# Regrouping the RWKV layer of a two-layer decoder kernel: two head groups half a step apart in the scan, key norms four tiles at a time, and GpSimd's work moved away from the first inversion

## The chip, the cores and the metric

The kernel runs on one core of one Trainium2 chip. The metric is the device time of one execution in microseconds (us); with one core that is the time of this core. The engines are named as in the profile: PE is TensorE (PEld its weight loads), DVE is VectorE, ACT is ScalarE, POOL is GpSimd and SP is SyncE, whose queue starts most of the transfers.

## The reference

The reference is a two-layer decoder trunk on 512 tokens of 1024 values. Layer 0 mixes tokens by a gated projection and a gated recurrence and ends in a dense SwiGLU. Layer 1 is an RWKV-7 time mixing of 16 heads of 64, then a top-2-of-8 mixture of experts. The change touches the time mixing alone:

```
    r = xr @ w_r ;  k = xk @ w_k ;  v = xv @ w_v        # xr, xk, ... mix a token with the one before it
    kk = heads(k * k_k)
    kk = kk / jnp.maximum(jnp.sqrt(jnp.sum(kk * kk, axis=-1, keepdims=True)), 1e-12)
    k = heads(k * (1.0 + (a - 1.0) * k_a))
    decay = jnp.exp(-jnp.exp(heads(w_log)))
    def step(s, inp):                                   # over 512 tokens, s is 64 x 64 for each head
        r_t, w_t, k_t, v_t, kk_t, b_t = inp             # b = kk * a
        s = (s * w_t[:, :, None, :]
             - jnp.einsum('bhvk,bhk->bhv', s, kk_t)[..., None] * b_t[:, :, None, :]
             + v_t[..., None] * k_t[:, :, None, :])
        return s, jnp.einsum('bhvk,bhk->bhv', s, r_t)
    ...                                                 # group norm of y per head (ln_g, ln_b), + bonus * v
    y = (y * g) @ w_o
```

## The kernel before, in words

The kernel is one program for one core. Layer 0 comes first, the RWKV layer lies between about 560 and 1040 us of the execution, and the expert layer, which streams its weights, takes the rest. A scheduler in the framework sets each engine's order from the order in which the code is written; `after(x, y)` pins an instruction behind another.

The recurrence is done in 8 chunks of 64 tokens (NCH = 8), and the 16 heads in two groups of 8 (`hf` 0 and 1), each group being 4 tiles of 128 channels. The stages that matter here, in order:

- **Key stage.** For each of 8 key tiles (128 channels, two heads), `key1` (L779 to 795) multiplies by w_k on PE (24 matmuls of 128x512), squares the result on ACT, splits the square in a rounded and a remaining part (`hi` on ACT, `lo` on POOL, L791). `key2` (L797 to 809) sums both parts over each head with 8 small matmuls (L800) and takes the reciprocal root by a chain of small DVE and ACT instructions. `key3` (L826 to 837) spreads it back with 4 matmuls (L831) and scales the tiles on POOL (L835) and DVE (L836, L837). `bonus_z` multiplies r by k on POOL (L816), and `bonus` sums it on PE (L823). Between and behind the tiles stands the first half of the v projection (`v_mm`, L867, 24 matmuls for each of 4 quarters of the sum).
- **Flips and flops.** For every chunk but the last and each group, `flip` scales a block of keys (POOL L847, for some chunks ACT) and `flop` transposes it on PE (L853) and writes it to DRAM, from where the scan reads it (`load_kt`).
- **Scores.** `scores(th)` (L937 to 981) makes, for chunks 0 to 3 (th = 0) and 4 to 7 (th = 1) and both groups, the products within a chunk (L956) and copies them out of PSUM with a causal mask: for th = 0 by DVE multiplications (L969, L970), for th = 1 by ACT copies (L962 to 967) and three affine selects on POOL (L976).
- **Inversions.** `invert(th)` (L985 to 1007) inverts 128 triangular 32x32 blocks on DVE: a transpose (L988), then 31 columns of a multiplication (L997) and a subtraction (L1001), both with two inputs in SBUF, then two transposes (L1004, L1006). `merge1` and `merge2` (L1027 to L1044) join the blocks to 64x64 ones by small matmuls on PE.
- **Scan.** `slot(s)` (L1257 to 1274) does for every chunk four steps on PE (L1141 and L1146, L1159, L1175, L1195) with ACT and DVE copies between; DVE adds the new state (L1181, L1183 for the first chunk), and POOL multiplies it by the decay (L1188). The two groups go through a step together, group 1 one chunk behind group 0, so that there are 9 slots. Behind each step stand `fill`s: dense matmuls of other work (the second half of v, then the gate matmuls L1244 to 1246, then the output projection L1308). `norm` (L1208 to 1237) is the group norm: POOL L1224, L1215 and L1216, DVE L1218 to L1237. Its factors come by four loads of `ln_gb` (L1353), which are issued in slot 4.

## Time and profile before

| | us |
|---|---|
| median of 3 runs (1482.36 to 1485.77) | 1482.56 |
| the profiled execution's own time | 1484.26 |
| its span in the trace | 1482.6 |
| PE busy in the span | 1383.6 (93%) |
| DVE busy | 993.4 (67%) |
| ACT busy | 807.1 (54%) |
| POOL busy | 334.4 (23%) |

The profiled execution is 1.7 us above the median. The table gives shares of the whole span, and the kernel's stages differ: from the profile's slices PE is busy 9 tenths or more nearly everywhere, but falls to between 3 and 8 tenths in slices 18 to 23 (about 670 to 890 us), which hold the key stage, the scores and the inversions. The mean granted TensorE clock is 0.958 of full speed; what is missing is missing between about 740 and 960 us.

### The profile page before, as it was taken

How to read it: one execution, taken by the hardware profiler on the slowest of the kernel's cores; microseconds unless marked ns; L12 is line 12 of the kernel's file. 1: busy time of each engine (PE TensorE's matmuls, PEld its weight loads, DVE VectorE, ACT ScalarE, POOL GpSimd, SP SyncE). 2: the span in 40 equal slices, each digit the busy share in tenths (PEclk: the TensorE clock that was granted, in tenths of full speed). 3: DMA queues.
4: the chain of work that ended last, by engine and by line, in shares of the span. 5: the costliest groups of instructions: out<-in, count | busy, mean ns of one | idle time of the engine just before them, and what ended most of it. 6: DMA issues, size and time to landing. Idle time of an engine off the chain costs nothing.

```text
span 1482.6 us, 31313 instructions
## 1 busy us (share of the span) xinstructions
PE 1383.6 (93%) x12567; PEld 1090.9 (74%) x12567; DVE 993.4 (67%) x1684; ACT 807.1 (54%) x1291; POOL 334.4 (23%) x375
## 2 busy tenths in 40 slices
PE   7999999999999999999878399898989999999995
PEld 5776788888888544654445267777889999999995
DVE  6643574544444433596679965675998998898885
ACT  4841444332233332396548435354778888888872
POOL 4000002000000012202532522642324322431323
PEclk9999999999999999999988768899999999999997
DMA  4220222223223433243122124245989999999983
GB/s 172 86 72 29 86 80 92 91 93 100 99 88 98 119 102 107 60 154 114 57 71 86 45 74 132 85 161 192 368 297 371 369 406 352 373 353 399 342 331 130
DMA packets 77109, 253.39 MB, mean 171 GB/s; under 512 B 9130, under 2 KB 9258, under 8 KB 76956
## 3 DMA queue, kind: packets, MB, share of 16 engines
q1 hardware_dynamic: 69824, 232.82, 44.6%
q0 software_dynamic: 3136, 10.62, 2.4%
q10 hardware_dynamic: 3996, 7.88, 1.4%
q8 instruction: 100, 1.64, 0.5%
q14 instruction: 53, 0.43, 0.1%
HBM read 235.12 MB, written 16.16 MB: 169 GB/s over the span
## 4 chain that ended last, share of the span: by engine, by line
PE 75%; DVE 13%; issue 4%; POOL 3%; ACT 2%; DMA 2%; ACTq 0%; DVEq 0%; SPq 0%; POOLq 0%
PE ps L264 8%; PE ps L263 8%; PE ps L265 8%; PE ps L1800 7%; PE ps L1801 7%; PE ps L1799 7%; PE ps L245 3%; PE ps L247 3%; PE ps L246 3%; DVE xs L997 2%; DVE xs L1001 2%; PE ps L1308 1%; PE ps L1923 1%; PE ps L867 1%; PE ps L278 1%
## 5 line engine op out<-in xcount | busy, mean ns | idle before, releaser
L226 ACT ACTIVATE whi<-wraw 128x1024 fp32r<-128x1024 f32 x95 | 100.6, 1059 | 276.1 <-PE ps L264 125.9
L264 PE MATMUL ps<-xg,whi 128*128 128x512 f32 x544 | 216.4, 399 | 3.8 <-DVE xg L326 3.7
L263 PE MATMUL ps<-xg,whi 128*128 128x512 f32 x544 | 216.8, 399 | 1.0 <-ACT xg L325 1.0
L265 PE MATMUL ps<-xg,wlo 128*128 128x512 f32 x544 | 216.5, 398 | 0.0
L1722 DVE SCALAR_TENSOR_TENSOR wlo<-eraw,wlo 128x1024 f16<-128x1024 f32 x125 | 154.3, 1234 | 12.5 <-ACT wlo L1721 11.5
L1722 DVE SCALAR_TENSOR_TENSOR whi<-eraw,whi 128x1024 f16<-128x1024 f32 x124 | 152.6, 1231 | 14.3 <-ACT whi L1721 14.1
L227 DVE TENSOR_TENSOR wlo<-wraw,whi 128x1024 fp32r<-128x1024 f32 x95 | 118.9, 1252 | 48.6 <-ACT whi L226 47.4
L1721 ACT ACTIVATE wlo<-eraw 128x1024 f16<-128x1024 f32 x125 | 131.9, 1055 | 24.4 <-PE ps L1801 10.0
L1721 ACT ACTIVATE whi<-eraw 128x1024 f16<-128x1024 f32 x124 | 130.7, 1054 | 15.7 <-PE ps L1801 12.5
L1901 POOL TENSOR_TENSOR hh<-su,hh 128x138 f16<-128x138 f32 (+5 forms) x77 | 82.1, 1067 | 218.8 <-ACT hh L1900 216.7
L1801 PE MATMUL ps<-xe,whi 128*128 128x138 f16 (+6 forms) x704 | 126.9, 220 | 3.9 <-DVE whi L1722 2.9
L1800 PE MATMUL ps<-xe,wlo 128*128 128x138 f16 (+6 forms) x704 | 127.5, 221 | 0.5 <-issue 0.5
L1799 PE MATMUL ps<-xe,wlo 128*128 128x138 f16 (+6 forms) x704 | 127.6, 221 | 0.3 <-issue 0.3
L1799 PE MATMUL ps<-xe,whi 128*128 128x138 f16 (+6 forms) x704 | 127.7, 221 | 0.0
L1800 PE MATMUL ps<-xe,whi 128*128 128x138 f16 (+6 forms) x704 | 127.6, 220 | 0.1
L1801 PE MATMUL ps<-xe,wlo 128*128 128x138 f16 (+6 forms) x704 | 127.1, 221 | 0.4
L264 PEld LDWEIGHTS ps<-xg,whi 128*128 128x128 f32 x544 | 102.8, 189 | 31.4 <-DVE xg L326 6.5
L263 PEld LDWEIGHTS ps<-xg,whi 128*128 128x128 f32 x544 | 103.3, 190 | 25.2 <-ACT xg L325 1.4
L265 PEld LDWEIGHTS ps<-xg,wlo 128*128 128x128 f32 x544 | 103.1, 189 | 24.2 <-issue 0.5
L1801 PEld LDWEIGHTS <-whi 128*128 128x128 f16 x1008 | 98.2, 97 | 9.1 <-DVE whi L1722 5.6
L286 POOL TENSOR_TENSOR tmp<-tmp 128x512 f32<-128x512 f32 x21 | 34.5, 1641 | 302.4 <-ACT tmp L284 249.5
L1800 PEld LDWEIGHTS <-wlo 128*128 128x128 f16 x1016 | 99.3, 98 | 2.2 <-issue 2.1
(521 smaller groups left out, 3423.4 us busy)
## 6 DMA issues: line engine op xcount, KB each, us to landing
eraw<-in_e_w SPq DMA_DIRECT2D x260, 512.0 KB
wraw<-in_ffn_g SPq DMA_DIRECT2D x22, 512.0 KB
wraw<-in_ffn_u SPq DMA_DIRECT2D x22, 512.0 KB
wraw<-in_ffn_d SPq DMA_DIRECT2D x16, 512.0 KB
wraw<-in_w_oo SPq DMA_DIRECT2D x13, 512.0 KB
wraw<-in_w_mo SPq DMA_DIRECT2D x8, 512.0 KB
wraw<-in_w_rk SPq DMA_DIRECT2D x8, 512.0 KB
wraw<-in_w_k SPq DMA_DIRECT2D x8, 512.0 KB
```

The source lines that it names most:

```text
L226: nc.scalar.activation(hi, raw, AF.Copy)
L227: nc.vector.tensor_sub(lo, raw, hi.bitcast(F32))
L245: nc.tensor.matmul(ps, w[:, 0, j], xh, start=(k == 0), stop=False)
L263: nc.tensor.matmul(ps, hi[:, j], xh, start=(k == 0), stop=False)
L264: nc.tensor.matmul(ps, hi[:, j], xl, start=False, stop=False)
L265: last = nc.tensor.matmul(ps, lo[:, j], xh, start=False, stop=(k == ktot - 1))
L1721: nc.scalar.activation(w[:, 0], raw, AF.Copy, scale=2048.0)
L1722: low = nc.vector.scalar_tensor_tensor(w[:, 1], raw, 2048.0, w[:, 0], op0=OP.mult, op1=OP.subtract)
L1799: nc.tensor.matmul(ps, w[:, 0, j], x[:, 0, k], start=(k == 0), stop=False)
L1800: nc.tensor.matmul(ps, w[:, 0, j], x[:, 1, k], start=False, stop=False)
L1801: nc.tensor.matmul(ps, w[:, 1, j], x[:, 0, k], start=False, stop=(k == n - 1))
L1901: nc.gpsimd.tensor_sub(hh[:, 1, f], u, hh[:, 0, f])
```

## The change

- The squares come straight from PSUM, without the split into two parts. The sums over heads of four key tiles go into one PSUM tile (`sums`, 4 fp32 matmuls for each tile, L802 of the changed kernel), and the chain of the reciprocal root runs twice, for tiles 0 to 3 and 4 to 7.
- All 14 flips are on POOL and in the key stage or in `scores(0)`; they use the ring of two `xs` buffers that the first inversion needs, too. The flops of group 1 stand in `scores(0)` and `scores(1)`.
- The 24 affine selects of `scores(1)` are gone. In their place stand 16 multiplications by the mask on POOL (L1002, L1003), held behind the first inversion by a copy of the mask on DVE (L1116).
- The third quarter of v's first half moves into `scores(0)`, the fourth stays with `scores(1)`. Of v's second half 48 matmuls stand beside the first inversion, 16 in the first merge, and the rest at the start of the scan.
- In the scan each group goes through its step alone, group 1 half a chunk behind group 0, in 8 half-steps of a slot; the fills behind a half-step are 2, then 1 in slots 1 to 5, then 4. So the gate matmuls are used up in slots 1 and 2.
- The loads of `ln_gb` are issued in slot 1.

The diff, cut to its core:

```diff
 def key1(n):
+            nc.scalar.activation(sq, pk, AF.Square, scale=kkc[:, n:n + 1])
             nc.scalar.activation(kk, pk3, AF.Copy, scale=kkc[:, n:n + 1])
-            nc.scalar.activation(sq.rearrange("p (i s) -> p i s", i=NTT), kk, AF.Square)
-            hi, lo = xs()
-            nc.scalar.activation(hi, sq, AF.Copy)
-            nc.gpsimd.tensor_sub(lo, sq, hi.bitcast(F32))
...
+        def sums(n, pre=None):
+            g, j = divmod(n, 4)
+            if not j:
+                pqs[g] = self.ps()[:64, :128]
+            z = sqs.pop(n)
+            for i in range(NTT):
+                r0 = 8 * j + 2 * i
+                mm = nc.tensor.matmul(pqs[g], indw[:, 30 - r0:94 - r0], z[:, i * 128:(i + 1) * 128], start=(j + i == 0),
+                                      stop=(j == 3 and i == NTT - 1))
...
-                    if th:
-                        for z, j, qs in ((BS[hf][c], 0, (0, 1)), (ak.rearrange("p a b t -> p (a b) t"), 1, (e,))):
-                            for q in qs:
-                                z_ = z[64 * q:64 * q + 64]
-                                nc.gpsimd.affine_select(z_, z_, pattern=[[0, 8], [1, C]], base=-j, channel_multiplier=-1,
-                                                        compare_op=OP.is_ge, fill=0.0)
...
+        def mask(hf, c):
+            nc.gpsimd.tensor_mul(a, a, msk[nat, 1:2, :].to_broadcast([64, 8, C]))
+            nc.gpsimd.tensor_mul(z, z, msk[:, 0:1, :].to_broadcast([128, 8, C]))
...
         run(inv)
+        after(nc.vector.tensor_copy(msk, msk), inv_end[0])
         inv = invert(1)
-        run(inv, 2)
+        run(inv, 12)
+        fill(None, 48 - vdone[0])
...
-        def slot(s, gs, counts, rate):
-            chains = [(hf, s - hf) for hf in range(NH) if 0 <= s - hf < NCH]
-            for f, n in zip((step1, step2, step3, step4), counts):
-                mm = f(chains)
+        def slot(s, gs, count, rate):
+            for f, hf, c in ((step1, 0, s), (step3, 1, s - 1), (step2, 0, s), (step4, 1, s - 1),
+                             (step3, 0, s), (step1, 1, s), (step4, 0, s), (step2, 1, s)):
+                if not 0 <= c < NCH:
+                    continue
+                mm = f([(hf, c)])
...
-            slot(s, ..., ((6, 6, 4, 4), (6, 6, 4, 4), (6, 6, 4, 4), (6, 6, 4, 4), (2, 2, 1, 1), (2, 2, 1, 1), (12, 12, 0, 0), (12, 12, 0, 0), (6, 6, 0, 0))[s], (2, 2, 2, 2, 1, 1, 1, 1, 1)[s])
+            slot(s, ([inv, mk], [inv, mk], [inv, mk], [join], ...)[s],
+                 (2, 1, 1, 1, 1, 1, 4, 4, 4)[s], 1)
```

POOL before, from the last flip of the key stage on: the first inversion's fills of its tile (MEMSET xs), then selects and flips up to the second inversion's fill (cut behind the first rows).

```order
L990 MEMSET xs 128x1024
L991 MEMSET xs 128x32
L847 TENSOR_TENSOR tmp<-KB,pe 128x512
L976 AFFINE_SELECT bs<-bs 64x512 x2
L976 AFFINE_SELECT ak<-ak 64x512
```

The same place in the changed kernel: `ak` and `bs` are the masked scores, `nt` and `S` the merge's and the scan's tiles.

```order
L850 TENSOR_TENSOR xs<-KB,pe 128x512 x7
L1013 MEMSET xs 128x1024
L1014 MEMSET xs 128x32
L1129 MEMSET S 64x8x64 x4
L1055 MEMSET nt_6449 32x32x32 x2
L1055 MEMSET nt_6448 32x32x32 x2
L1002 TENSOR_TENSOR ak<-ak,msk 64x512
L1003 TENSOR_TENSOR bs<-bs,msk 128x512
L1002 TENSOR_TENSOR ak<-ak,msk 64x512
L1013 MEMSET X 128x1024
```

Between the fills of the two inversions' tiles there is no flip and no select any more; 16 mask multiplications now stand from there up to the first decay multiplication of the scan.

DVE before, in the second inversion's columns (L997 the multiplication, L1001 the subtraction; the last factor of a shape is the column's number), where the first states of the scan's group 0 are copied (L1183):

```order
L997 TENSOR_TENSOR xs<-xs,X 128x7x18 x2
L1001 TENSOR_TENSOR X<-X,xs 128x7x18 x2
L997 TENSOR_TENSOR xs<-xs,X 128x7x19
L997 TENSOR_TENSOR xs<-xs,X 128x6x19
L1183 COPY S<-ps 64x4x64 x2
L1001 TENSOR_TENSOR X<-X,xs 128x7x19
```

The same copy in the changed kernel (L1201, with L1020 and L1024 for the columns):

```order
L1020 TENSOR_TENSOR xs<-xs,X 128x5x22 x2
L1024 TENSOR_TENSOR X<-X,xs 128x5x22 x2
L1201 COPY S<-ps 64x4x64 x2
L1020 TENSOR_TENSOR xs<-xs,X 128x5x23
L1020 TENSOR_TENSOR xs<-xs,X 128x4x23
L1024 TENSOR_TENSOR X<-X,xs 128x5x23
```

It stood within column 19 and now stands behind column 22; group 1's copy now stands behind column 27.

PE before, in slots 4 and 5 of the scan: `L1141` opens a slot, `dual` names the gate matmuls.

```order
L1141 MATMUL ps<-S,RK 128x128 x8
L1146 MATMUL ps<-vu,ak 64x64 x16
L1246 MATMUL ps<-X,dual 128x512
L1244 MATMUL ps<-X,dual 128x512
L1159 MATMUL ps<-tmp,nt_6533 64x64 x16
L1245 MATMUL ps<-A_6720,dual 128x512
L1246 MATMUL ps<-X,dual 128x512
L1175 MATMUL ps<-vu,kt 64x64 x16
L1195 MATMUL ps<-vu,bs 64x64 x16
```

The same place in the changed kernel (L1159 and L1164 for L1141 and L1146, then L1177, L1193, L1213):

```order
L1193 MATMUL ps<-vu,kt 64x64 x8
L1159 MATMUL ps<-S,RK 128x128 x4
L1164 MATMUL ps<-vu,ak 64x64 x8
L1213 MATMUL ps<-vu,bs 64x64 x8
L1177 MATMUL ps<-tmp,nt_6448 64x64 x8
L1213 MATMUL ps<-vu,bs 64x64 x8
L1159 MATMUL ps<-S,RK 128x128 x4
L1164 MATMUL ps<-vu,ak 64x64 x8
```

Each step has half as many matmuls, steps of the two groups alternate, and no gate matmul stands between them.

## Rows read from the trace of the kernel before

**Rows 1.** The page: the span, and the chain of work that ended last, by engine as a share of the span.
```profile
span 1482.6 us, 31313 instructions
PE 75%; DVE 13%; issue 4%; POOL 3%; ACT 2%; DMA 2%; ACTq 0%; DVEq 0%; SPq 0%; POOLq 0%
```
**Rows 2.** Two stretches of 20 us. Columns: the stretch, its length, busy us (and instructions) of PE, PEld, DVE, ACT and POOL, the granted clock, the DMA share, GB/s.
```profile
740.00:760.00 20.00, 15.38 (x86) 8.93 (x85) 13.45 (x23) 9.01 (x20) 10.85 (x9) 0.84 0.16 53
820.00:840.00 20.00, 6.50 (x53) 4.12 (x51) 20.00 (x54) 10.20 (x32) 11.45 (x14) 0.78 0.17 65
```
**Rows 3.** The chain of waits in the key stage, in order of time: start, length, what.
```profile
730.38 2.48 POOL tmp L816 x2
732.86 1.23 POOL xs L791
...
740.77 2.47 POOL tmp L816 x2
```
**Rows 4.** PE in order of time from the last key tile to the first scores: start, length, what, and the idle time before it with its releaser.
```profile
745.58 0.95 PE L823 MATMUL ps<-indr,tmp 128*128 128x2 f32 x8
...
748.16 5.35 PE L867 MATMUL ps<-whi,xn 128*128 128x512 f16 x24
...
780.62 3.46 PE L956 MATMUL ps<-RK,KB 64*128 64x128 f32 x32
```
**Rows 5.** DVE in order of time: the first and last copies of `scores(0)`, then the first inversion's first column, one in its middle, the last one, and its last transpose.
```profile
783.61 0.42 DVE L969 TENSOR_TENSOR bs<-ps,msk 128x256 f32<-128x256 f32 x1 [0.31 <-ACT A L964]
...
797.01 0.43 DVE L970 TENSOR_TENSOR ak<-ps,msk 64x256 f32<-64x256 f32 x1
...
799.54 0.27 DVE L997 TENSOR_TENSOR xs<-xs 128x16 f32<-128x16 f32 x2
...
820.20 2.57 DVE L1001 TENSOR_TENSOR xs<-xs 128x135 f32<-128x135 f32 x2
...
841.73 0.21 DVE L1001 TENSOR_TENSOR xs<-xs 128x31 f32<-128x31 f32 x1
...
843.74 1.85 DVE L1006 STREAM_TRANSPOSE X<-xs 128x1024 f32<-128x1024 f32 x1
```
**Rows 6.** Two stretches chosen by what stands in them, columns as in rows 2: the middle of the first inversion, and the scan from the middle of slot 3 to slot 4.
```profile
810.69:833.49 22.80, 12.16 (x108) 7.75 (x105) 22.80 (x37) 17.79 (x57) 19.20 (x24) 0.95 0.19 70
```
```profile
913.00:934.00 21.00, 21.00 (x322) 19.97 (x321) 3.07 (x6) 7.27 (x12) 2.47 (x4) 0.51 0.28 90
```
**Rows 7.** DVE in order of time in the second inversion (th = 1), whose columns have the same shapes as the first one's.
```profile
849.74 1.05 DVE L997 TENSOR_TENSOR xs<-xs,X 128x16 f32<-128x16 f32 x2 [2.15 <-POOL X L991]
...
852.08 1.84 DVE L1036 COPY nt<-xs 32x1024 f32<-32x1024 f32 x2
...
863.64 0.66 DVE L1001 TENSOR_TENSOR X<-X,xs 128x135 f32<-128x135 f32 x2
...
866.62 2.80 DVE L1001 TENSOR_TENSOR X<-X,xs 128x126 f32<-128x126 f32 x2
...
882.16 0.88 DVE L1183 COPY S<-ps 64x256 f32<-64x256 f32 x2 [12.25 <-PE ps L1175]
883.07 1.16 DVE L1001 TENSOR_TENSOR X<-X,xs 128x133 f32<-128x133 f32 x2
...
892.92 0.21 DVE L1001 TENSOR_TENSOR X<-X,xs 128x31 f32<-128x31 f32 x1
```
**Rows 8.** Groups of POOL instructions between 690 and 1000 us: line, operation, tiles, shapes, count, busy us, mean ns of one, idle time before them and its releasers.
```profile
L1188 POOL TENSOR_TENSOR SP<-S,pe 64x256 f32<-64x256 f32 x24 | 18.9, 787 | 47.3 <-DVE S L1181 32.6 <-DVE S L1183 13.5
L1216 POOL TENSOR_TENSOR tmp<-tmp,xn 128x512 f32<-128x512 f32 x8 | 12.1, 1512 | 0.5
L847 POOL TENSOR_TENSOR tmp<-KB,pe 128x512 f32<-128x512 f32 x11 | 12.1, 1098 | 16.3 <-PE ps L853 11.3 <-DVE xn L712 4.7
L976 POOL TENSOR_SCALAR_AFFINE_SELECT bs<-bs 64x512 f32<-64x512 f32 x16 | 11.7, 732 | 26.7 <-ACT bs L966 25.9
```
**Rows 9.** PE in order of time in the scan: the openings of slots 1, 2, 4 and 6 (L1141; one step of the other kind, L1146, beside them), the start of the second merge (L1027), and one wait.
```profile
884.97 1.05 PE L1141 MATMUL ps<-S,RK 128*128 128x128 f32 x8
...
896.23 2.04 PE L1141 MATMUL ps<-S,RK 128*128 128x128 f32 x16 [1.15 <-DVE S L1181]
898.20 1.15 PE L1146 MATMUL ps<-vu,ak 64*64 64x64 f32 x32
...
910.04 2.11 PE L1027 MATMUL ps<-xs,A 32*32 32x32 f32 x64
...
928.32 3.78 PE L1141 MATMUL ps<-S,RK 128*128 128x128 f32 x16
...
949.44 0.69 PE L1175 MATMUL ps<-vu,kt 128*64 128x64 f32 x16 [2.66 <-ACT vu L1163]
...
952.19 3.03 PE L1141 MATMUL ps<-S,RK 128*128 128x128 f32 x16
```
**Rows 10.** The chain of waits in slots 3 to 5: start, length, what.
```profile
921.90 14.00 issue
...
937.15 1.29 POOL bs L1224
```
**Rows 11.** One group of DVE instructions of the norms between 690 and 1000 us, columns as in rows 8.
```profile
L1235 DVE TENSOR_TENSOR bs<-bs,gvar 128x512 f32<-128x512 f32 x4 | 6.3, 1586 | 0.4 <-DVE gvar L1234 0.4
```

More of the change, by code (lines that the diff above doesn't have):

```diff
@@ L777, in rwkv, with run @@
         bon = self.bon
-        prods, rns = {}, {}
+        sqs, pqs, rns = {}, {}, {}
+        def run(g, n=999):
+            for _ in range(n):
+                if next(g, "end") == "end":
+                    return
         def key1(n):
@@ L1008, in invert @@
             yield
-        def run(g, n=999):
-            for _ in range(n):
-                if next(g, "end") == "end":
-                    return
         S_ = [(b, e) for b in range(2) for e in range(2)]
@@ L1329, in out0 @@
             yield from out_mm(0, A, done)
-        load_vu(0, 0)
-        load_kt(0, 0)
-        load_kt(1, 0)
-        for mm, n in zip(merge(0), (2,) * 8):
-            fill(mm, n)
+        for hf in range(NH):
+            load_vu(hf, 0)
+            load_kt(hf, 0)
+        for mm in merge(0):
+            fill(mm, 2)
+            run(inv, 1)
         g2 = [scp.tile([128, D], F32R, name=name, bufs=2) for name in ("X", "A21")]
@@ L1341, in rwkv, with masks @@
         join = iter(())
+        def masks():
+            for c in range(4, NCH):
+                for hf in range(NH):
+                    mask(hf, c)
+                    yield
+        mk = masks()
         for s in range(NCH + 1):
-            if s == 3:
-                run(inv)
-                join = merge(1)
-            if s == 4:
+            if s == 1:
+                fill(None, 96 - vdone[0])
                 run(dense)
@@ L1353, in rwkv @@
                         nc.sync.dma_start(z[b], bass.AP(tensor=src.tensor, offset=src.offset + j * D + b * 512, ap=[[0, 128], [1, 512]]))
-                for i in (2, 3):
-                    t = self.t()
-                    nc.scalar.activation(t, pv[i], AF.Copy, scale=cm[:, 0:1])
-                    nc.sync.dma_start(v_d[i * 128:(i + 1) * 128, 512:], t)
+            if s == 3:
+                run(inv)
+                join = merge(1)
+            if s == 4:
+                run(mk)
+                run(join)
             if s == 6:
```

225 lines of the change are left out of this document (114 added, 111 removed).

## The prediction

> **What bounds the kernel now.** I read the page first, then the stretches of 20 us through the RWKV layer, then the chain of waits and each engine's order of time where a stretch showed a new limit. On the page PE holds 75% of the chain that ended last and DVE 13% [rows 1]: nearly everything is matmuls in a row, and only where PE waits for another engine is there time that a new order can win. The stretches show where. In the key stage PE is busy for 15.38 of 20 us, and in the first inversion for 6.50 of 20, with DVE at 20.00 [rows 2]. In the late key tiles the chain runs over POOL: r times k (2.48 us), then the remainder of the squares (1.23), and the next tile's pair comes 10.39 us after the last one [rows 3], while PE's own work in such a tile is 5.35 for 24 matmuls, 0.95 for the bonus [rows 4] and about half a microsecond of small ones (an estimate from these). In the first inversion the chain is DVE alone, from the first column at 799.54 to the last transpose's end at 845.59 [rows 5]. From there PE is full again, but partly at half clock: in 913 to 934 it is busy for 21.00 of 21 us at a granted clock of 0.51, its lower level of 1.2 GHz [rows 6]. Behind the scan the expert layer streams weights and only moves as a whole with the scan's end.
>
> **A. Key stage and scores: 0.** The new tile has no remainder on POOL and runs the root's chain for four tiles at once. Then a tile takes PE's 6.9 us instead of 10.4; v's first matmuls could begin about 5 us earlier, and one quarter of v (5.35 us [rows 4]) leaves the stage, so the scores begin perhaps 14 us before 780.6. But this is not passed on. `scores(0)` took 13.8 us of DVE copies [rows 5] and now has a v quarter and seven flops between, some 18 us (13.8, and 5.35 that partly overlaps). And the inversion's two buffers are those of the flips: its first column must wait until the last flops of group 1, which stand inside `scores(1)`, have read them, where I add 10 us. So 766 + 4 (first matmuls) + 18 + 10 + 2 (transpose) gives 800, where 799.5 was: 0. Bounds: -8 if `scores(0)` keeps its 13.8 and half of the wait goes, +4 if POOL's flips hold PE in the key stage.
>
> **B. The first inversion: -16.3.** 31 columns took 799.54 to 841.94, less a weight split of 1.2 between them, 41.2 us. The second inversion has the same shapes: from 849.74 to 893.13, less the wait and copies of the scan's state (13.2), the merge's copies (1.9), and what the columns at 849.74, 866.62 and 883.07 have over their like (0.8, 2.1 and 0.5), it took 24.9 [rows 7]. The column of 135 elements was 2.57 in the first and 0.66 in the second [rows 5, 7]. What differs is POOL: 19.20 of 22.80 us busy in the first's middle [rows 6] with selects and flips. All of these have left; 41.2 - 24.9 = 16.3. I take it whole, since a DVE weight split is still between; the bound on the other side is 10, if flips are late.
>
> The page "SBUF — State Buffer" of the Trainium skill ("Who interferes with whom") says that a DVE instruction with two SBUF inputs contends with a GpSimd instruction that reads SBUF, each holding a shared pair of ports for its whole length. The slow columns agree, and the rule speaks against the next part.
>
> **C. From the inversion's end to slot 1: -2.** It was 845.59 to 884.97 [rows 5, 9], 39.4 us. Now 16 mask multiplications run on POOL beside the second inversion, 8 of 128x512 and 8 of 64x512. The nearest rows are 1.10 for a flip of 128x512 and 0.73 for a select of 64x512 [rows 8]; I take 1.10 and 0.92 (between the two, as it has two inputs), 16.2 us. What POOL costs DVE: 24 selects and 6 flips, 24.1 us by the same rows, cost 16.3, so 0.68 of their time, and 16.2 cost 11. Before the first state copy stand now 22 columns instead of 19: 18.7 of the 24.9 us, and 1.9 transpose, 1.9 merge copies, the 11, the copy 0.9 and some 3 of start and first decay: 37.4. Bounds: +5 more if the masks cost their whole 16.2, so +3; -6 where they cost nothing and PE's merge sets the time.
>
> **D. Slots 1 and 2: -5.** A slot's own matmuls are 2.04 and four times 1.15, 6.6 us at full clock [rows 9]. From 884.97 to 910.04, 25.1 us, stood two slots, the first step of the third and some 40 v matmuls. Now only 12 gate matmuls remain between (0.22 each by the 24 in 5.35 [rows 4]): 13.2 + 3.1 + 2.7, and 1 for the first states, 20. Below, -6 without that wait; above, +13 if the clock falls to half here (38).
>
> **E. The second merge and slots 3 to 5: +2.5.** 910.04 to 952.19 was 42.2 [rows 9]. There is a stall in the chain, 14.00 us up to POOL's first norm multiplication, which waited for the late `ln_gb` loads [rows 10]; PE worked through it, and POOL's work that jammed behind it then held PE at 949.44 for 2.66. This goes. But the gate matmuls go, too. At half clock the opening of slot 4 took 3.78 instead of 2.04 [rows 9], so about twice; the merge's 256 matmuls take 15.3 (their 8 x 1.9 at half), the rest of slot 3 6.9 and slots 4 and 5 13.2 each, 48.6. The first few us come before the clock falls, -4: 44.6. Bounds: 48.6 (+6.4), and 24.3 at full clock (-18).
>
> **F. Slots 6 to 8 and what follows: -2.** 20 more of the output matmuls stand in the scan, 4.4 us that are missing behind it; net 0. Of POOL's and DVE's jam at the norms I give back 2. Bounds -6 and +4. Moved at no cost: the new POOL preparation of index tiles, the state loads and `kbt_d` stores, on queues that stand far ahead; if that cover fails, a load delays one slot's step.
>
> **Sum.** 0 - 16.3 - 2 - 5 + 2.5 - 2 = -22.8, against the profiled execution's 1484.3: 1461.5. That execution is 1.7 above the median, so 1460.
>
> **The rivals.**
> 1. *The clock stays up (1440).* With two independent chains PE never waits in slots 3 to 5, the clock holds 2.4 GHz, and E is -18 instead of +2.5: 20 less. For it: before, a pair of slots with few gates ran at full clock in part. Against it: PE without a gap in 913 to 934, and the clock at 0.51 [rows 6]; the new slots hold the same small matmuls.
> The page "TensorE: Matmul & The Clock Gate" of the Trainium skill ("HAM oscillation — how this bites in real kernels") puts a falling clock down to gaps in which PE idles; by that rule this rival is what happens. The row of 913 to 934 disagrees.
> 2. *The time is given back at the inversion's start (1472).* The change doesn't free the first inversion: the flops that release its buffers stand behind ACT's copies of `scores(1)`, whose selects waited for ACT for 25.9 us over 16 [rows 8]. Three such parts late, the first column starts at 811, and B's gain is halved by 12.
> 3. *Two queues a slot (1489).* Each group now updates its state alone. Where DVE holds a norm piece of 1.59 [rows 11] and POOL one of 1.51 ahead of a decay multiplication [rows 8], each update waits behind one of each, twice a slot instead of once, 3.1 us more in each of 9 slots: +28, if nothing covers it, 1460 + 29. It decides if PE idles over 2.5 us a slot from slot 1 on (22.8 / 9). Against it: in a half-step the other group's matmuls stand between, and the norms fill only slots 4 to 8.
>
> **How the numbers follow.** Forecast 0.60, the clock 0.20, given back 0.12, two queues 0.08. A change under 0.3% (4.4 us) could not be told from none. Forecast and clock are faster in nearly all of their width, given back in most: 0.85 faster; 0.07 within 0.3%, from the edges of the forecast and rival 2; 0.08 slower. The range reaches from rival 1 (1437) to the far side of rival 2 (1478); it leaves out rival 3 and the far ends of the sum.
>
> **What would show it.** In the new profile: key tiles 7 us apart on PE; the first column at about 800 and 31 columns in some 26 us; columns of the second inversion of 1.5 to 2.5 us beside the masks; slot 1 about 37 us behind the first inversion; a granted clock near 0.5 in slots 3 to 5; no 14 us before the first norm multiplication. The forecast is wrong if the first inversion's columns still last 40 us, if it starts ten us later, or if PE has idle gaps through the scan.

## The result and the profile after

The changed kernel takes 1499.48 us (median of 7 runs, 1496.72 to 1503.50), the kernel before 1484.64 beside it: a ratio of 1.0100, 95% interval 1.0076 to 1.0124. It is slower by 1%; the forecast was 1460, with a range from 1437 to 1478.

The page of the changed kernel; its profiled execution took 1497.78 us:

```profile
span 1496.1 us, 31249 instructions
PE 1418.3 (95%) x12563; PEld 1121.0 (75%) x12563; DVE 987.4 (66%) x1661; ACT 796.6 (53%) x1262; POOL 334.0 (22%) x357
```

PE is busier by 34.7 us than in the kernel before (1383.6) and executes about the same matmuls: the same work has become longer. DVE has lost 6 us. I read the terms of the sum in the order of time, from the engine that ends each.

PE of the changed kernel in order of time, in the key stage (L802, L829), at the first scores (L978), and in the scan, where L1159 opens the step of a group, L1164 is the step's other half, and L1045 begins the second merge. The trace counts each of these fp32 matmuls as two, so that the 16 of a step of both groups in the order of the program are 32 here, and the 8 of one group 16:

```profile
748.70 1.09 PE L802 MATMUL ps<-tmp,indw 128*64 128x128 f32 x8 [2.37 <-ACT tmp L789]
...
754.76 1.87 PE L829 MATMUL ps<-indr,tmp 128*128 128x2 f32 x8 [4.65 <-POOL tmp L822]
...
773.52 2.06 PE L978 MATMUL ps<-RK,KB 64*128 64x128 f32 x32
...
878.01 1.13 PE L1159 MATMUL ps<-S,RK 128*128 128x128 f32 x8 [1.86 <-DVE S L1201]
...
894.64 1.05 PE L1159 MATMUL ps<-S,RK 128*128 128x128 f32 x8
...
903.03 1.14 PE L1164 MATMUL ps<-vu,ak 64*64 64x64 f32 x16
...
908.41 1.19 PE L1045 MATMUL ps<-xs,A 32*32 32x32 f32 x32
...
927.70 2.08 PE L1159 MATMUL ps<-S,RK 128*128 128x128 f32 x8
...
945.22 2.04 PE L1159 MATMUL ps<-S,RK 128*128 128x128 f32 x8 [2.33 <-DVE S L1199]
...
963.76 2.08 PE L1159 MATMUL ps<-S,RK 128*128 128x128 f32 x8
```

DVE of the changed kernel: the first and the last mask copy of `scores(0)` (L991, L992), the start of the first inversion (L1011, L1020), its column of 135 elements and its last column and transpose, one column of the second inversion, the first state copy (L1201), and then slot 4, where L1199 is the state's sum and L1253 to L1255 are pieces of the norms:

```profile
778.49 0.41 DVE L991 TENSOR_TENSOR bs<-ps,msk 128x256 f32<-128x256 f32 x1
...
796.11 0.43 DVE L992 TENSOR_TENSOR ak<-ps,msk 64x256 f32<-64x256 f32 x1
...
801.79 1.97 DVE L1011 STREAM_TRANSPOSE xs<-X 128x1024 f32<-128x1024 f32 x1 [3.79 <-PE ps L856]
806.14 0.27 DVE L1020 TENSOR_TENSOR xs<-xs 128x16 f32<-128x16 f32 x2 [2.38 <-POOL xs L1014]
...
817.51 0.65 DVE L1024 TENSOR_TENSOR xs<-xs 128x135 f32<-128x135 f32 x2
...
831.89 0.21 DVE L1024 TENSOR_TENSOR xs<-xs 128x31 f32<-128x31 f32 x1
...
833.90 1.87 DVE L1029 STREAM_TRANSPOSE X<-xs 128x1024 f32<-128x1024 f32 x1
...
847.38 1.42 DVE L1020 TENSOR_TENSOR xs<-xs,X 128x45 f32<-128x45 f32 x2
...
876.99 0.87 DVE L1201 COPY S<-ps 64x256 f32<-64x256 f32 x2
...
938.01 0.42 DVE L1199 TENSOR_TENSOR S<-ps,SP 64x256 f32<-64x256 f32 x1
...
940.22 1.51 DVE L1254 TENSOR_TENSOR bs<-bs,tmp 128x512 f32<-128x512 f32 x1
941.66 1.75 DVE L1253 TENSOR_TENSOR bs<-bs,gvar 128x512 f32<-128x512 f32 x1
...
944.64 0.43 DVE L1199 TENSOR_TENSOR S<-ps,SP 64x256 f32<-64x256 f32 x1
```

The scores start at 773.52 where they started at 780.62 [rows 4], but the first column at 806.14 where it was 799.54 [rows 5]. The first inversion now has the pace of an undisturbed one: 0.65 for the column that took 2.57. Then the second is slow (1.42 for the multiplication of a column of 45 elements, which takes 0.35 where POOL is idle, e13 below), and the scan loses: slots 1, 2, 4 and 6 open at 878.01, 894.64, 927.70 and 963.76, against 884.97, 896.23, 928.32 and 952.19 [rows 9]. A lead of 7.0 us at slot 1 is a delay of 11.6 at slot 6.

Four windows of the changed kernel, columns as in rows 2; the first is the start of slot 1, the second is slot 2:

```profile
878.00:890.00 12.00, 11.99 (x88) 9.45 (x89) 9.90 (x38) 1.78 (x3) 2.69 (x5) 0.57 0.18 52
894.64:906.25 11.61, 11.61 (x149) 9.78 (x147) 7.23 (x11) 5.31 (x8) 3.81 (x4) 1.00 0.35 108
884.00:944.00 60.00, 57.78 (x799) 51.28 (x797) 26.87 (x47) 22.53 (x38) 18.36 (x19) 0.84 0.26 81
944.00:972.00 28.00, 25.42 (x183) 23.41 (x184) 15.30 (x25) 8.04 (x16) 14.26 (x14) 0.51 0.16 48
```

Of these the first and the last two in the kernel before:

```profile
878.00:890.00 12.00, 12.00 (x146) 7.68 (x144) 7.78 (x31) 3.44 (x6) 1.28 (x2) 0.95 0.15 35
884.00:944.00 60.00, 58.48 (x925) 48.44 (x923) 33.04 (x82) 28.65 (x47) 16.23 (x20) 0.83 0.36 114
944.00:972.00 28.00, 22.79 (x299) 19.17 (x298) 24.31 (x37) 13.58 (x24) 19.50 (x19) 0.94 0.23 70
```

From 884 to 944 the clocks are alike (0.84 and 0.83), but from 878 to 890, where slot 1 begins in the changed kernel, it is 0.57 for 0.95. Behind the wait at 945.22 the changed kernel is at the half level for 28 us, where it was 0.94, and executes 183 PE instructions where it was 299.

| term | forecast | measured | how (us) |
|---|---|---|---|
| A, to the first column | 0 | +6.6 | 806.14 - 799.54 |
| B, first inversion | -16.3 | -16.4 | 29.6 for 46.05, to the end of its last transpose |
| C, to slot 1 | -2 | +2.9 | 42.2 for 39.4 |
| D, slots 1 and 2, to the merge | -5 | +5.3 | 30.4 for 25.1 |
| E, merge and slots 3 to 5 | +2.5 | +13.2 | 55.35 for 42.15 |
| F, the rest | -2 | +1.9 | remainder of 1496.1 - 1482.6 = 13.5 |

### The profile page after: what moved, and what is told of

The parts are those of the page before. It is cut to its first block, busy times and chain, and to the rows that moved or that the text cites. A ratio compares the mean times of both kernels' runs of the same rounds, so it can differ in the third digit from the quotient of the medians.

```text
span 1496.1 us, 31249 instructions
## 1 busy us (share of the span) xinstructions
PE 1418.3 (95%) x12563; PEld 1121.0 (75%) x12563; DVE 987.4 (66%) x1661; ACT 796.6 (53%) x1262; POOL 334.0 (22%) x357
## 5 line engine op out<-in xcount | busy, mean ns | idle before, releaser
L1740 ACT ACTIVATE whi<-eraw 128x1024 f16<-128x1024 f32 x124 | 130.7, 1054 | 15.6 <-PE ps L1820 11.6
```

The costliest lines, as they stand in the source:

```text
L1740: nc.scalar.activation(w[:, 0], raw, AF.Copy, scale=2048.0)
```

## The experiments

The two theories at the start. **Pairs:** before, the two groups' 64x64 matmuls stood in turns and ran beside each other, and the changed scan runs each group's alone. **Queues and fills:** the regrouped scan loses by what stands between its steps (the norms' pieces ahead of the state's sum, the places of the dense fills), and by the clock that falls behind it. A row of the kernel before bears on the first: slot 8, in which one group is alone.

```profile
984.50 1.14 PE L1146 MATMUL ps<-vu,ak 64*64 64x64 f32 x16
```

16 matmuls take 1.14 there, and 32 of both groups took 1.15 in slot 2 [rows 9]. All ratios below are to the kernel before, run on the same chip, with 95% intervals. The runs stand on several chips; a difference between two runs is that of their medians, and the difference of their ratios, in microseconds, is given beside it where the two disagree.

### The pairs: e1, e2, e10, e16

`e1_before_unpaired` is the kernel before, `e10_old_scan_unpaired` is `e6` below and `e16_new_fills_unpaired` is `e2`, each with the two loops of three steps exchanged:

```diff
-            for hd, hs in enumerate(heads):
-                for hf, c in chains:
+            for hf, c in chains:
+                for hd, hs in enumerate(heads):
```

`e2_after_paired` is the changed kernel with both groups in one step again, its fills and norms at the changed pace:

```diff
+        def slot(s, gs, counts, rate):
+            chains = [(hf, s - hf) for hf in range(NH) if 0 <= s - hf < NCH]
+            for f, n in zip((step1, step2, step3, step4), counts):
+                mm = f(chains)
...
+                 ((4, 4, 4, 4), (2, 2, 2, 2), (2, 2, 2, 2), (2, 2, 2, 2), (2, 2, 2, 2), (2, 2, 2, 2), (8, 8, 4, 4), (8, 8, 4, 4), (6, 6, 0, 4))[s], 2)
```

> The kernel before, and in the scan's steps with 64x64 matmuls (L1146, L1159, L1195) the loop over the two head groups outside the loop over the heads: the same instructions in the same step, but the 8 matmuls of group 0, then the 8 of group 1, instead of in turns. Pairing theory (in turns, two neighbours run side by side on PE, since the groups are a chunk apart and so use opposite halves; alone they don't): each of the three steps takes 2 x 1.14 instead of 1.15 us at full clock, 3.4 us in each of 7 joint slots, 24 us, more where the clock is at half: 1500 to 1515, and the step's rows 2.2 us long. Clock theory (the changed kernel is slower since no dense matmuls stand in slots 3 to 5) and queue theory (each group waits alone behind DVE's and POOL's norm pieces): no change here, 1480 to 1487, since fills, steps and the other engines' orders are those of before.

> The changed kernel with the scan's slot as before: both groups go through a step together, group 1 a whole chunk behind, and the fills of two half-steps behind a step (64 output matmuls in slots 6 to 8, 12 gate matmuls in slots 1 and 2, as in the changed kernel). Pairing theory: 24 to 30 us less than the changed kernel's 1499.5, so 1470 to 1476, under the kernel before. Clock theory: still no dense matmuls in slots 3 to 5, so 1490 to 1500, with the granted clock at 0.5 there. Queue theory: one update per slot instead of two, some 10 to 15 less, 1485 to 1490.

> The same run with the old scan (1471.9), with the two groups' 64x64 matmuls one group after the other inside a step, as in the first run of the kernel before. Pairing theory: 1.90 instead of 1.15 us a step, 2.25 in each of 7 joint slots, 15.8 on PE, 10 to 16 in the time: 1482 to 1488. That would leave 12 to 18 of the 27.6 between it and the changed kernel to the half-steps' own order and the clock. If pairing is worth nothing here, 1470 to 1474; if it is all, 1495 or more.

> Whole steps with the changed kernel's fills (1500.2 with pairs), and the pairs broken. If pairing costs here what it costs elsewhere, 10 to 15 more, 1510 to 1516; the changed kernel's 1499.5 would then be 10 to 15 under it, which is what half-steps win by their order. If there is no difference to 1500.2, pairs are worth nothing where the clock is at half and PE waits, and half-steps win nothing.

Measured: e1 1493.46, ratio 1.0066 (1.0036 to 1.0097); e10 1486.25, 1.0016 (0.9993 to 1.0039), 14.3 over e6; e2 1500.19, 1.0111 (1.0080 to 1.0142); e16 1504.64, 1.0133 (1.0094 to 1.0173), 4.5 over e2. PE in e1:

```profile
899.43 1.90 PE L1146 MATMUL ps<-vu,ak 64*64 64x64 f32 x32
```

1.90 for the 1.15 of the same 32 matmuls: the pairs are real, and worth 10 to 14 us in the old scan (e1, e10). Not all of that is matmul time. Slot 3 of e6, then of e10, columns as in rows 2:

```profile
902.34:918.83 16.49, 16.49 (x409) 14.23 (x407) 6.22 (x10) 9.76 (x17) 4.57 (x6) 1.00 0.38 128
906.07:930.49 24.42, 24.42 (x410) 21.25 (x408) 6.10 (x10) 9.65 (x16) 3.81 (x6) 0.72 0.25 77
```

About the same matmuls take 7.9 us longer here, at a granted clock of 0.72 for 1.00; slot 1 takes 15.8 for 11.7 at 0.56 for 0.86, and slot 2, at full clock in both, 10.5 for 9.3. So more than half of e10's 14.3 stands in slots 1 and 3, beside a lower clock. e1 lies below the 1500 to 1515 of its pairing theory.

But e2 has the pairs and is no faster than the changed kernel. The pairs alone, by which it was to come to 1470 to 1476, are refuted as the whole cause. In e2 PE waits, up to 5.36 us at once, for the state's sum on DVE. There pairs are worth 4.5 us by the medians and 3.3 by the ratios (e16), and as the two intervals overlap, it isn't shown that they are worth anything.

### The fills' place: e5, e6, e7, e15

`e5_after_fills_late` keeps the half-steps and puts v's matmuls in slots 0 to 3 and the gates in slots 4 and 5 again; with them the loads of `ln_gb` go back to slot 4. `e6_after_old_scan` is the changed kernel with the scan of before: joint steps, as in e2, fills (two behind a step in slots 0 to 3, since fewer of v's matmuls are left for them), loads, and norms at the old pace. `e7_before_no_gates_45` is the kernel before without fills in slots 4 and 5 (they run behind). `e15_v_early` is e6 with v's matmuls drained at slot 1.

```diff
 (e5, e6)
-            if s == 1:
+            if s == 4:
                 fill(None, 96 - vdone[0])
 (e5)
-                 (2, 1, 1, 1, 1, 1, 4, 4, 4)[s], 1)
+                 (1, 1, 1, 1, 1, 1, 4, 4, 4)[s], 1)
 (e6)
-                 (2, 1, 1, 1, 1, 1, 4, 4, 4)[s], 1)
+                 ((2, 2, 2, 2), (2, 2, 2, 2), (2, 2, 2, 2), (2, 2, 2, 2), (2, 2, 1, 1), (2, 2, 1, 1), (12, 12, 0, 0), (12, 12, 0, 0), (6, 6, 0, 0))[s], (2, 2, 2, 2, 1, 1, 1, 1, 1)[s])
 (e7: in slots 4 and 5)
-(2, 2, 1, 1), (2, 2, 1, 1)
+(0, 0, 0, 0), (0, 0, 0, 0)
 (e15, to e6)
-            if s == 4:
+            if s == 1:
                 fill(None, 96 - vdone[0])
                 run(dense)
+                dense = iter(())
+            if s == 4:
```

> The changed kernel with half-steps as they are, and the dense matmuls where they stood before: the last 32 of v one behind each half-step of slots 0 to 3, the gate matmuls one behind each in slots 4 and 5 (before: drained at the start of slot 1, gates in slots 1 and 2). Clock theory (slots 4 and 5 run at half clock for want of dense matmuls): slots 4 and 5, now 17.5 and 18.5 us long, come down to 12 to 14 each and the time by 8 to 12, 1487 to 1491. Pairing theory alone (what is lost is lost in the unpaired steps): the slots shrink by less than 3 and the time stays at 1496 to 1502. Queue theory (waits behind DVE's and POOL's norms): no change in slots 4 and 5 either, the idle time of PE before a step's state read stays at 2 us.

> The changed kernel with the whole scan as before: paired steps, group 1 a chunk behind, and fills as in the slots of before (32 of v in slots 0 to 3, gates in 4 and 5, output matmuls 12, 12, 0, 0 in 6 and 7 and 6, 6 in 8). What is left of the change are the key norms, the flips, the masks behind the first inversion and v's place. If the scan's regrouping and its fills cost the time, the gain of the stages before it shows: the first inversion ends about 10 us sooner than before and slot 1 opens 5 to 7 sooner, 1476 to 1480, faster than the kernel before. If the first stages gave nothing to the scan (masks on the second inversion eat it), 1483 to 1487; if something else in the change costs the time, 1490 or more.

> The kernel before without fills in slots 4 and 5: its 12 gate matmuls then stand in a row ahead of slot 6. Clock theory: the granted clock stays near 0.5 from slot 3 through slots 4 and 5, which become 13 to 16 us long each instead of 12.3 and 11.6, and with the gates' 2.7 us behind them the time rises by 5 to 10, 1488 to 1493. Without the clock the slots shrink by the gates' 4.8 us, and the time stays, 1480 to 1485. Pairing theory says nothing on it, since pairs stay.

> The run with the old scan (1471.9), with only v's last fills moved: they are all done at the start of slot 1, as in the changed kernel, and slots 1 to 3 have none; the gates stay in slots 4 and 5. If the absence of dense matmuls around the second merge is what brings the clock down (with the new fills and pairs the merge's slot took 24.7 us at a clock of 0.5, with v's fills 16.5 at 1.0), 8 to 14 more than 1471.9: 1480 to 1486. If it is the gates' place, 1472 to 1476, and 1500 comes from the gates.

Measured: e5 1508.00, 1.0148 (1.0120 to 1.0176); e6 1471.93, 0.9917 (0.9892 to 0.9942); e7 1484.12, 0.9995 (0.9978 to 1.0012); e15 1477.53, 0.9942 (0.9923 to 0.9960).

e6 says where the change loses: with the stages ahead of the scan as changed and the scan as before, it is 12 us faster than the kernel before and 27.6 faster than the changed one. The regrouping of the scan is the loss, the rest is a gain. PE in e6 at the opening of slot 1, and e6's window:

```profile
881.37 2.05 PE L1159 MATMUL ps<-S,RK 128*128 128x128 f32 x8 [11.94 <-DVE S L1201]
```

```profile
884.00:944.00 60.00, 54.80 (x1042) 45.21 (x1038) 37.27 (x66) 32.29 (x54) 27.83 (x29) 0.99 0.42 134
```

Here PE idles 11.94 us ahead of slot 1 and then runs at a clock of 0.99, where the changed kernel had 0.84. e5 with as many v fills a slot runs near half clock (0.54 from 916 to 944, PE without a gap) and came out slower than each of its theories said, and e7 with no gates loses nothing. The two windows of e5:

```profile
884.00:944.00 60.00, 60.00 (x701) 49.65 (x700) 22.04 (x54) 20.34 (x31) 8.75 (x12) 0.70 0.23 72
916.00:944.00 28.00, 28.00 (x324) 23.92 (x320) 3.45 (x5) 8.77 (x14) 2.45 (x4) 0.54 0.11 29
```

So neither the fills' density nor their place decides the clock by itself. Draining v early costs 5.6 by the medians and 3.7 by the ratios (e15), between its two expectations; the intervals of e15 and e6 overlap. In its trace slot 3 takes 20.1 us at a granted clock of 0.68, for 16.5 at 1.00 in e6.

### Turns between groups in half-steps: e11, e12

The changed kernel, with step 4 of one group and step 2 of the other written in turns, matmul by matmul, pinned with `after`:

```diff
+        def turns(h4, c4, h2, c2):
...
+            for hd, hs in enumerate(heads):
+                for do, args in ((do4, (mm4, h4, c4, hd, hs)), (do2, (mm2, h2, c2, hd, hs, p))):
+                    if do:
+                        last, mm = mm, args[0](*args[1:])
+                        if last is not None:
+                            after(mm, last)
```

`e11_after_turns_opposite` pairs step 4 of group 0 with step 2 of group 1, `e12_after_turns_same` the other way.

> The changed kernel with its half-steps, but the last two of a slot put in turns, matmul by matmul: step 4 of group 0 and step 2 of group 1, which write opposite halves of PSUM's partitions. Pairing theory: these 32 matmuls take 1.15 to 1.3 us together instead of 2.14 at full clock, 1 us a slot, twice at half clock, 8 to 10 in the time: 1489 to 1493. Queue and clock theories: 1497 to 1503.

> The same as the run before it, but the two put in turns are step 2 of group 0 and step 4 of group 1, which write the same half of PSUM's partitions. Pairing theory: no gain, since neighbours use the same columns of the array: 32 matmuls in 2.1 to 2.3 us, 1497 to 1503. If taking turns as such is what helps (fewer waits between a step and its copy), 8 less as in the run before it.

Measured: e11 1528.52, 1.0304 (1.0255 to 1.0354); e12 1535.68, 1.0341 (1.0297 to 1.0385). Both expectations failed. PE in e11, one such stretch (L1195 is step 4, L1186 step 2):

```profile
889.92 0.33 PE L1195 MATMUL ps<-vu,bs 128*64 128x64 f32 x2
890.18 0.33 PE L1186 MATMUL ps<-tmp,nt 64*64 64x64 f32 x2
890.43 0.33 PE L1195 MATMUL ps<-vu,bs 128*64 128x64 f32 x2
```

Each turn from one shape to the other costs: two matmuls (one fp32 matmul) every 0.26 us, which makes 4.1 for 32, an estimate from this spacing; the whole stretch took 5.4, as the clock fell to 0.50 within it. The two steps alone take 1.14 or 1.15 each. In the kernel before it was matmuls of equal shape that ran side by side. The Trainium skill says both: "TensorEngine Tiling (Array Packing)", section "Key Properties", has different tiles run in parallel, and changing the tiling mode, not just the tile, drain the engine. Both agree with the rows of e1 and e11.

### The norms' pace: e17, e18

In the changed scan `run(g, 1)` stands behind each of 8 half-steps; before, from slot 4 on, behind each of 4 steps. A norm has three pieces; so it is through behind the third of 8 half-steps, where it took three of 4 steps. `e17_after_norms_slower` sets that back in the changed kernel (in slot 8, where group 0 has no half-step, no norm advances), `e18_new_fills_norms_slower` does so in e2, by a rate of `(2, 2, 2, 2, 1, 1, 1, 1, 1)[s]` for its 2. The edit of e17:

```diff
                 for g in gs:
-                    run(g, rate)
+                    if s < 4 or not hf:
+                        run(g, rate)
```

> The changed kernel, with the norms of slots 4 to 8 advanced only behind group 0's half-steps, 4 pieces a slot as before instead of 8, so that on DVE the state sums stand ahead of the norms' last multiplications. If the state sum behind norm pieces is what stretches slots 4 and 5 (its wait, and the clock at half behind it), they come down from 17.5 and 18.5 to 13 to 15 and the time to 1488 to 1493. If the unpaired steps and the clock alone do it, 1496 to 1501.

> Paired whole steps with the changed kernel's fills (1500.2), and the norms at the pace of before in slots 4 to 8. If the norms' pace is the 22.7 us between that run and the one with v's fills early (1477.5), 1477 to 1482. If it is the gates, which are used up in slots 1 and 2, no change: 1497 to 1502. In between, its share.

Measured: e17 1487.44, 1.0043 (1.0021 to 1.0064), 12.0 under the changed kernel (8.5 by the ratios); e18 1483.19, 0.9994 (0.9970 to 1.0018), 17 under e2, and 11.3 over e6. In e17 DVE around the state's sum in slot 4, PE's openings of slots 5 and 6, and the window:

```profile
938.27 0.87 DVE L1199 TENSOR_TENSOR S<-ps,SP 64x256 f32<-64x256 f32 x2
...
940.44 3.44 DVE L1253 TENSOR_TENSOR bs<-bs,gvar 128x512 f32<-128x512 f32 x2
```

```profile
941.35 1.16 PE L1159 MATMUL ps<-S,RK 128*128 128x128 f32 x8
...
953.07 1.16 PE L1159 MATMUL ps<-S,RK 128*128 128x128 f32 x8
```

```profile
944.00:972.00 28.00, 25.02 (x284) 21.07 (x278) 23.69 (x37) 12.04 (x22) 17.47 (x16) 1.00 0.24 72
```

Both halves of the sum are done at once, ahead of the long norm pieces; in the changed kernel the second half came 6.6 us behind the first, behind them. The wait of 2.33 is gone, and so is the half clock from 944 to 972: a granted clock of 1.00 for 0.51, and slots 5 and 6 open at 941.35 and 953.07, for 945.22 and 963.76. The sign of this cause and its size, 8.5 to 12 here, are shown. That the wait brings the clock down is the order in time, not shown alone.

e18 has joint steps and norms as e6, and the fills of the changed kernel: their place (with the early `ln_gb` loads) costs the 11.3. Most of it stands in slot 3, here in e18, 24.9 us for e6's 16.5 above, at a clock of 0.63 for 1.00:

```profile
901.72:926.59 24.87, 24.06 (x405) 22.77 (x401) 5.51 (x10) 8.73 (x15) 5.00 (x8) 0.63 0.25 75
```

### Masks and flops: e3, e4, e8, e9, e13, e14

`e3_after_flops_early` puts two flops for one beside each score. `e4_after_no_masks` leaves out the causal mask of chunks 4 to 7; this changes the routing of the expert layer, so its whole time (1996.13) says nothing and only its trace ahead of the scan is used. `e8_before_masks` is the kernel before with the mask multiplications instead of the selects. `e9_old_scan_act_copy` is e6 with the first state copies on ACT. `e13_masks_late` is e6 with the masks held behind the second inversion and advanced in slots 2 and 3; the inversion's code is written whole ahead of slot 2 for it, no longer ahead of slot 3. `e14_masks_late_act_copy` is both.

```diff
 (e3)
-                flops(m, 1)
+                flops(m, 2)
 (e4, in mask)
+            return
 (e8)
-                                nc.gpsimd.affine_select(z_, z_, pattern=[[0, 8], [1, C]], base=-j, channel_multiplier=-1,
-                                                        compare_op=OP.is_ge, fill=0.0)
+            nc.gpsimd.tensor_mul(a, a, msk[nat, 1:2, :].to_broadcast([64, 8, C]))
+            nc.gpsimd.tensor_mul(z, z, msk[:, 0:1, :].to_broadcast([128, 8, C]))
 (e9, e14)
-                        nc.vector.tensor_copy(o, pst[d])
+                        nc.scalar.activation(o, pst[d], AF.Copy)
 (e13, e14: behind the first inversion, and now behind the second)
-        after(nc.vector.tensor_copy(msk, msk), inv_end[0])
...
+            if s == 2:
+                run(inv)
+                after(nc.vector.tensor_copy(msk, msk), inv_end[0])
```

> The changed kernel with two flops instead of one behind each of the four v pieces in the first scores, so that all flops of group 1 stand before the second scores and free the first inversion's buffers earlier. If the start of the first inversion is held by the last flop, the first column comes at 800 instead of 806 and the end 5 us earlier, 1494. If something behind hides it (the masks, the merge), 1498 to 1500.

> The changed kernel without the 16 mask multiplications on POOL; it leaves out the causal mask of chunks 4 to 7. If they cost the second inversion their whole length on DVE, as the columns between 843 and 862 look, the first state copy comes 12 us earlier and the time falls by 8 to 12, 1488 to 1492. If PE's first merge then sets the copy, 11 less at most. If the price is 0.68 of their length as before, the same size, 8 to 12. No effect on the scan's steps by any theory.

> The kernel before with one part of the change: the 24 selects of the second scores go, and 16 mask multiplications on POOL stand behind the first inversion, as in the changed kernel; flips, key norms, v and scan as before. By my price of 0.68 the 17.5 us of selects leave the first inversion 12 shorter, ended at 834 instead of 845.6; the 16 multiplications of 1.3 us then cost the second one 15 to 17 up to the first state copy, which ends at 880 to 884 against 882 before: 1480 to 1486, no gain. If the first inversion's gain is passed on, slot 1 opens 8 us sooner, 1474 to 1477.

> The run with the old scan on the changed stages (1471.9), and the first chunk's state copies on ACT instead of DVE. There PE was idle for 11.94 us ahead of slot 1, because the copy stood on DVE behind 22 columns of the second inversion, which the masks slow. If that queue is what delays slot 1, slot 1 opens some 11 us sooner, at 870, and most of it lasts to the end: 1461 to 1466. If the next state update waits on DVE in the same way (its sum L1199 stays there, behind the same columns), 3 to 5 of it remain: 1467 to 1469.

> The run with the old scan on the changed stages (1471.9), and the 16 masks held behind the second inversion instead of the first, so that they run on POOL in slots 2 and 3 and neither inversion has POOL beside it. If the masks are what slows the second inversion's columns (1.3 to 1.5 us where they were 0.3 to 0.5), the first state copy comes 9 to 12 us sooner and slot 1 opens at 870 to 872: 1460 to 1464. If POOL's masks then delay the decay multiplication in slots 2 and 3, half of it is given back: 1465 to 1468.

> The run before it, with the first chunk's state copies on ACT. With ACT alone slot 1 opened 7 us sooner but slot 2 only 2.4. If the second inversion is out of the way sooner, the sums of slot 1 aren't held on DVE any more, and ACT's copy adds 2 to 4: 1457 to 1461. If DVE isn't in the way any more, nothing: as the run before it.

Measured: e3 1504.78, 1.0152 (1.0102 to 1.0201); e8 1477.41, 0.9942 (0.9912 to 0.9972); e9 1472.62, 0.9905 (0.9870 to 0.9940); e13 1462.01, 0.9841 (0.9817 to 0.9864); e14 1460.90, 0.9833 (0.9803 to 0.9863).

e3 ends the first inversion 3 us earlier and opens slot 1 2.8 earlier, and gains nothing by it, with a time above both of its expectations: slot 1 is 3.7 longer, with 5.5 us of idle PE, and slot 3 is 4.4 longer at a granted clock of 0.66 for 0.84. e8 shows that the masks alone, in the kernel before, bring over half of e6's 12 us: 6.6 by its median, 8.6 by its ratio, with runs that scatter from 1467 to 1483. Its first inversion takes 33.8 us (799.54 to 833.33) for 46.05, so the selects alone cost 12.3 of B's 16.4. In e9 slot 1 opens 7 us earlier than in e6 and slot 2 only 2.4, and nothing is left at the end.

The first state copy on DVE in e4:

```profile
875.08 0.87 DVE L1200 COPY S<-ps 64x256 f32<-64x256 f32 x2 [4.58 <-PE ps L1192]
```

From the second inversion's first transpose to this copy e4 takes 29.4 us, 4.58 of them a wait for PE, and the changed kernel 41.1. So the masks cost DVE 16.3 us (41.1 less 24.8), and the path 11.7, because PE's merge stands behind. Of the 16.3, 3.2 lie ahead of the first column, where a copy is slower and DVE waits 2.25 for POOL's fill of the tile, which stands behind masks on POOL; 13.1 are slower columns. The two groups of the changed kernel's POOL (columns as in rows 8):

```profile
L1002 POOL TENSOR_TENSOR ak<-ak,msk 64x512 f32<-64x512 f32 x8 | 11.1, 1385 | 14.2 <-DVE msk L1116 13.9
L1003 POOL TENSOR_TENSOR bs<-bs,msk 128x512 f32<-128x512 f32 x8 | 10.3, 1282 | 0.3
```

They are busy for 21.4 us, so DVE loses 0.76 of what POOL takes. e13 takes that cost away, not by leaving the masks out but by moving them. DVE in e13, the second inversion's first columns and the first state copy:

```profile
842.24 0.26 DVE L1022 TENSOR_TENSOR xs<-xs,X 128x16 f32<-128x16 f32 x2 [1.15 <-POOL X L1016]
...
843.15 0.35 DVE L1022 TENSOR_TENSOR xs<-xs,X 128x45 f32<-128x45 f32 x2
...
867.16 0.88 DVE L1202 COPY S<-ps 64x256 f32<-64x256 f32 x2 [2.57 <-PE ps L1194]
```

The columns are as fast as in the first inversion, the copy waits for PE and not for DVE's queue, and slot 1 opens at 869.40 for e6's 881.37. Of these 12 us, 9.9 are left at the end (11.3 by the ratios). With the copy on ACT as well (e14) nothing more comes, as DVE is free there. e13 and e14 beat both kernels: 1462.01 is 24.8 below the kernel before beside it, and 37 below the changed one.

## Why the prediction was wrong

**The failed step is in D: "A slot's own matmuls are 2.04 and four times 1.15, 6.6 us at full clock", carried over to half-steps.** 1.15 is the time of 32 matmuls of two groups side by side. A group alone takes 1.14 for its 16, so a slot of two half-step chains costs 1.14 or 1.15 twice in three of its steps. Rows 9 gave the 32; the row at 984.50 above, which I did not read, gave the 16, and the two together say it. The changed kernel's slot 2 shows it, with PE never idle at a granted clock of 1.00: of its 11.6 us four gate matmuls take 0.43 each, and the other 9.9 are the slot's own matmuls, 3.3 more than my 6.6.

D missed by 10.4, 30.4 for 20. Twice 3.3 is 6.6 of that. The 12 gate matmuls took 0.43 each between small matmuls, not the 0.22 of matmuls in a row, 2.5 more. With both at these prices 3.3 of slot 1's 16.6 us are left over, and slot 1 began at a clock of 0.57, which I had only as a bound. The third slot's first step and the first states came out 1.9 lower together.

**E failed by another mechanism, which I had under rival 3 but put in the wrong place.** I said that the state's sum would wait behind norm pieces, priced it by two queues a slot in each of 9 slots, and excused it because "the norms fill only slots 4 to 8". It is the pace that decides: the norms advanced twice as fast in those slots. E missed by 10.8, of which slots 4 and 5 are 9.7 (17.5 and 18.5 for 13.2 each). With the slower norms of e17 they take 13.3 and 11.7. That their sum of 25.0 meets my 26.4 is luck: I had paired steps at half clock, and these are single ones at 0.75 and 1.00. The pace cost 12.0 us (e17; 8.5 by the ratios), by few waits (PE waits for 6.65 us in all from 870 to 1010) and a clock at 0.51 for 28 us behind the one at 945.22. By my own condition, 2.5 us of idle PE in every slot from 1 on, rival 3 is not what happened.

**What each part of the regrouping costs depends on the others.** From e6 to the changed kernel is 27.6. Going there by single steps, the place of the fills costs 11.3 (e18), the norms' pace 17.0 more (e2), and half-steps for joint steps then nothing that can be told from noise (1500.19 to 1499.48). With the slower norms half-steps cost 4.2 over e18, or 7.3 by the ratios (e17), and in the old scan the separation costs 14.3 (e10). So a sum of e10's 14.3 and e17's 12.0 is near 27.6 by chance.

**A: wrong by 6.6, beyond its bound of +4.** I had the scores start at 766; they start at 773.52. PE waits 2.37 for ACT's squares and 4.65 for POOL's products of r and k in the key stage: POOL is busy for 13.18 of the 20 us from 740 to 760 (10.85 before [rows 2]). `scores(0)` took the 18 us that I gave it (778.49 to 796.54), and the waits for the last flops (3.79) and POOL's fill of the tile (2.38) are in the 10 I had put aside.

**B: right,** -16.4 for -16.3, and by the cause named: with POOL's selects and flips gone, the columns are as short as the second inversion's, and with the selects alone gone 12.3 of it is there (e8).

**C: wrong sign, right mechanism.** The masks' time on POOL was 21.4 for my 16.2, and DVE lost 0.76 of it rather than 0.68: 16.3 for 11, about the 5 by which C missed. This was the bound that I had at +3.

**E's other part, the reading of the 14 us, was wrong.** I took the stall ahead of the first norm multiplication [rows 10] for late `ln_gb` loads. They are issued at 870.8 to 872.8 now, and a stall of 10.40 stays; in the kernel before they were issued from 892.8 to 900.9, long before the multiplication at 937.15. The chain of waits of the changed kernel, and ACT in order of time:

```profile
922.74 10.40 issue
933.14 1.27 POOL bs L1242
```

```profile
931.77 0.59 ACT L1169 ACTIVATE tmp<-ps 64x512 f32<-64x512 f32 x1 [3.38 <-PE ps L1164]
932.38 0.63 ACT L1241 ACTIVATE tmp<-bs 128x512 f32<-128x512 f32 x1
```

POOL's multiplication starts when ACT's square of the norm (L1241) is done, at 933.01, and that stands on ACT behind slot 4's copy L1169, which waits for PE. The stall is an order on ACT, and no load.

**F: +1.9 for -2,** within its bounds of -6 and +4. "20 more of the output matmuls" was miscounted (64 in the scan now, 60 before); it was net 0 in the sum.

**Rivals 1 and 2.** The clock did not stay up (0.84 from 884 to 944). The inversion's start was later, 806.14 and not the 811 of rival 2, and that was not the loss. In the sums of the rivals 3 and 1 two figures don't fit: 9 times 3.1 on 1460 is 1488, not 1489, and the range starts at 1437, below rival 1's 1440.

**Left open** is why the clock falls in some slots. In e6 it is 0.99 from 884 to 944 with PE busy for 54.80 of 60 us, in e5 0.70 with 60.00, and removing the gates in e7 moved nothing. Much of what e10, e15 and e18 lose to e6 stands in slot 3, at a clock of 0.72, 0.68 and 0.63 for 1.00. I can tell what the two levels cost, but not from the code which one a stretch will get.

## What to carry to other kernels

Before splitting a joint step in two, look for the step in which one part is already alone (a first or last slot), and compare its time with the joint one: if 16 take as long as 32, the halves ran beside each other. When a generator that is advanced once a step gets twice the steps, its pieces come twice as fast, and stand in front of whatever shares their engine. POOL's selects and flips cost DVE's first inversion and the masks its second one about the same, some 16 us: move such work behind the stage and not from one to the next (e13). When several changes touch one stage, undo them one at a time from both ends: the same exchange of loops cost 14.3 us in the old scan (e10) and 4.5 at most by the medians beside the changed fills and norms (e16).

## What the runs showed that I had not expected

- 64x64 matmuls of two groups in turns: 32 in 1.15 us at full clock, and 16 alone in 1.14. In the other order, 32 in 1.90 (e1). Turns between a 128-row and a 64-row shape: two every 0.26 us (e11).
- A POOL multiplication of 64x512 by a broadcast mask took no less than one of 128x512: 1.385 and 1.282 us on the mean.
- DVE lost 16.3 us in the second inversion to 21.4 us of POOL multiplications beside it. With the same multiplications behind it, the multiplication of a column of 45 elements took 0.35 for 1.42.
- PE without a gap for 28 us at a granted clock of 0.54 (e5, 916 to 944), and with gaps at 0.99 (e6, 884 to 944).
- A gate matmul of 128x512 alone between small matmuls took 0.43 us of PE's time at full clock (slot 2 of the changed kernel), and in a row 0.23 (974 us).
